# A two-block transformer kernel: the first block's TensorE order written by hand, cheaper sums, and 512-column down projections

## The chip, the cores and the metric

One core of one Trainium2 chip runs the whole program. The metric is device time in microseconds (us) of one execution. In the text PE is TensorE (PEld its weight loads), DVE is VectorE, ACT is ScalarE, POOL is GpSimd, and SP is SyncE, which here only issues DMAs. L340 is line 340 of the kernel before.

## The reference

The model works on 256 tokens of width 1024 (batch 1), all in fp32. The first block has three branches on one normed input: an RWKV-7 recurrence (8 heads of 64), a stick-breaking attention (8 heads of 64) and an attention to 256 memory rows (4 heads of 128). Their gated sum goes through an output projection, and a convolutional feed-forward of width 2816 follows. The second block is an mLSTM mixer, a feed-forward, a block attention and a third feed-forward. Cut to what the change touches:

```python
# first block
h = rms_norm(x, norm1_g)
p_rwkv, p_sb, q_mem, gate_logits = split(h @ w_in)
y_a = rwkv7_branch(p_rwkv, ...)                # a recurrence over the 256 tokens
y_b = stick_breaking_branch(p_sb, q_g, k_g)    # log_between = reversed cumsum(log_1mb) - log_1mb
y_m = memory_branch(q_mem, mem, mem_g, ...)    # softmax over the 256 memory rows
merged = sum(sigmoid(gate_logits) * einsum('btnc,ncd->btnd', stack(y_a, y_b, y_m), w_branch))
x = x + merged @ w_out
# a feed-forward: one in the first block, two in the second
hp = conv3(rms_norm(x, g) @ w_up)
x = x + (silu(gate) * val) @ w_down            # the down projection, 2816 x 1024
```

## The kernel before

Activations are held with features on partitions: a tile is 128 features by 256 tokens, and an input of width 1024 is 8 such tiles (k = 0 to 7). Every large product is done in two fp32r halves: `split` (L307) writes hi = fp32r(x) on ACT and lo = x - hi on DVE, and `mm3` (L334) adds three passes into one PSUM tile: whi with xh, whi with xl, wlo with xh (L340 to L342, 256 columns each). Products that are wanted with tokens on partitions go through `tp_group` (L356): there the activation is the stationary operand and 512 weight columns move (L363 to L365), six passes for each k, and one such step uses four weight tiles.

All weights are one stream of tiles of 128 x 128 in the order of use, eight to a DMA of 512 KB on SP's queue. `Stream.take` hands out the next tile and keeps two groups ahead: DMA into `wstg` (three buffers), then hi on ACT (L237) and lo on DVE (L238), three buffers each. The first block uses 656 tiles: memory keys and values (64), RWKV projections (112), queries, keys and values of memory and stick heads (128), then for each of three branches 8 x (8 gate + 4 branch) tiles (288) and the output projection (64). After that come up projections (352 tiles each) and down projections (176 each) of three feed-forwards, and the mixers of the second block.

The kernel is built in a framework that works out the order of each engine itself: it simulates the program and lets each engine take what it expects to be ready, with earlier program lines first. Nothing before fixes the order of PE. Semaphores follow from data, and every engine then runs its own list strictly in order.

What stands in the way of the stream in the first block: `Stats` (norms: squares are added on ACT and DVE, `_rows` L425 sums over partitions with one-column fp32 matmuls L429, `_spread` L437 copies the result over partitions with an fp32 matmul, L440); `qk_feat` (per-head norms and transposes); `run_rwkv` (for four pairs of heads `rw_prep` and `rw_scores`, then 64 x 64 triangular inverses, whose 16 x 16 diagonal blocks are solved on DVE after a trip through DRAM by DMAs of SP (L698 to L712), two doubling steps with `rw_lt`, `rw_lz`, `rw_lx`, then four chunks of the recurrence); the memory heads (`me_scores`, `me_values`); the stick heads in four pairs (L888 to L922: scores, the cumulative sum `sb_c` as three fp32 products, the weighted values `sb_o`). A plain fp32 matmul shows as two records (passes) in the trace, a transpose and an fp32r matmul as one. PSUM has eight banks in three pools: `acc` four, `pm` two, `pr` two.

The down projection is the last branch of `residual` (L939): for each of 8 output tiles `fp_tile` runs 22 x 3 passes over the separate tiles `ffh` and `ffl`, and one DVE add (L945) puts the result on the running state `xt`.

Of the kernel before, what the change touches and what calls it, by code (L numbers as in the profile page):

```python
# [16 lines left out]
T = 256  # L17
# [9 lines left out]
STARTS = (82, 148, 181, 247, 279)  # L27
HEAD = 4
# [162 lines left out]
def body(tc, a, out, voff, coff, tap=None, upto=99):  # L191
# [68 lines left out]

    warm = cpool.tile([128, 1], F32, name="warm")
# [42 lines left out]
    pw = ps_r("warm_ps")  # L304
    for _ in range(10):
        PE.matmul(pw, wz[:, 0:128], wz, start=True, stop=True)

# [26 lines left out]
    def mm3(o, X, k, w, start, stop, **kw):  # L334
        hi, lo = w
        if isinstance(X.H, list):
            xh, xl = X.H[k], X.L[k]
        else:
            xh, xl = X.H[:, k], X.L[:, k]
# [16 lines left out]
    def tp_group(X):  # L356

        po = [ps_acc(), ps_acc()]
        for k in range(KD):
            hi, lo = W.take(4)  # L360
            for tt in range(2):
                s = slice(tt * 128, (tt + 1) * 128)
                PE.matmul(po[tt], X.H[:, k, s], hi, start=(k == 0), stop=False)  # L363
                PE.matmul(po[tt], X.L[:, k, s], hi, start=False, stop=False)  # L364
                PE.matmul(po[tt], X.H[:, k, s], lo, start=False, stop=(k == KD - 1))  # L365
        return po
# [27 lines left out]
    class Stats:  # L394
# [83 lines left out]
    s4tag = dict(mkT="s4a", mv="s4b", mqT="s4c", sqT="s4d", skT="s4e", sv="s4b", macc0="s4c", macc1="f1")  # L478
# [4 lines left out]
    def qk_feat(X, st, nh, gain, name, po=None):  # L483
        po = po or tp_group(X)
        rs = head_rs(po, nh, st and st.ev, name)
        dst = s4(name)
        for tt in range(2):
            qn = normed(po, tt, rs, nh, name + "n")
            tok_to_feat(qn, dst, tt, gain)
        return dst  # L490

    def v_tok(X, st, name):
        po = tp_group(X)
        dst = s4(name).rearrange("p a t -> p (a t)").rearrange("p (a c) -> p a c", c=512)
# [3 lines left out]

    W.fill(0)
# [6 lines left out]
    pmk = tp_group(XM)  # L506
    sm._rows()
# [5 lines left out]
    for k in range(KD):  # L513
        V.scalar_tensor_tensor(x0[:, k], x0[:, k], vec("norm1_g", k), s1.bc, op0=OP.mult, op1=OP.mult)
        split(X1.H[:, k], X1.L[:, k], x0[:, k])

    mkT = qk_feat(XM, sm, 4, vec("mem_k"), "mkT", pmk)
    mv = v_tok(XM, sm, "mv")

# [67 lines left out]
    def rw_prep(p, rs, SC, BK, UV, wc):  # L587
# [28 lines left out]
        PE.matmul(pb[:, T:2 * T], con("bones"), sx, start=True, stop=True)  # L616
# [5 lines left out]
        for par in range(2):  # L622
# [5 lines left out]
            V.tensor_tensor(BK[s, p, :, o], ch(kp, par), ch(iw, par), op=OP.mult)  # L628
        pvt = ps_r("rw_pvt")
# [32 lines left out]
    def run_rwkv():  # L662
# [61 lines left out]
        for b in (16, 32):  # L724
# [6 lines left out]
            for h in range(2):  # L731
                pz = mm("rw_lz", tms[h], Zu[h])
# [3 lines left out]
                V.tensor_tensor(Zu[h], Zu[h], pz, op=OP.add)  # L736

        Y = krt[0][:, 0:4].rearrange("p c (q v) -> p c q v", v=64)
        Sw = None
        for c in range(4):  # L740
# [8 lines left out]
            A.activation(P_[64:128], pp4[64:128, :, 1], AF.Copy)  # L749
            pu = ps_r("rw_puu")  # L750
# [6 lines left out]
            A.activation(UV[64:128, :, c, 1], puv[64:128], AF.Copy)  # L757
            if c < 3:
# [30 lines left out]
            V.tensor_copy(Y[0:64, c], pp4[0:64, :, 1])  # L789

# [12 lines left out]
        YA = Half("yA", "b")  # L803
# [24 lines left out]
        return YA  # L828
# [13 lines left out]

    YA = run_rwkv()


    mqT = qk_feat(X1, None, 4, gains[:, 1:2], "mqT")
    YM = Half("yM", "a")

    def me_scores(h):
# [5 lines left out]
        for tt in range(2):  # L855
            PE.matmul(ps2[:, tt], mqT[:, h, tt * 128:(tt + 1) * 128], mkT[:, h], start=True, stop=True)
# [7 lines left out]
    def me_values(h, pr_):  # L864
        pt = ps_m("me_t")
        pt2 = pt.rearrange("p (m t) -> p m t", t=T)
        for mt_ in range(2):
            for tt in range(2):
                PE.transpose(pt2[:, mt_, tt * 128:(tt + 1) * 128], pr_[:, tt, mt_ * 128:(mt_ + 1) * 128], ident)
        pT = mp.tile([128, 2, T], F32, name="me_pT", bufs=1)  # L870
        A.activation(pT, pt2, AF.Copy)
        po_ = ps_m("me_o")
        for mt_ in range(2):
            PE.matmul(po_[:, :T], mv[:, mt_, h * 128:(h + 1) * 128], pT[:, mt_], start=(mt_ == 0), stop=(mt_ == 1))
        split(YM.H[:, h], YM.L[:, h], po_[:, :T])
        dbg(f"ym{h}", YM.H[:, h].bitcast(F32))

    sqT = qk_feat(X1, None, 8, gains[:, 0:1], "sqT")
    pr_ = me_scores(0)
    for h in range(4):  # L880
        pn_ = me_scores(h + 1) if h < 3 else None
        me_values(h, pr_)
        pr_ = pn_


    skT = qk_feat(X1, None, 8, vec("sb_k"), "skT")
    sv = v_tok(X1, None, "sv")
    YB = Half("yB", "e")  # L888
    for p in range(4):
        ze = mp.tile([128, 4, 384], F32, name="sb_ze", tag="sbt")  # L890
        z, e = ze[:, 0:2], ze[:, 2:4]
        pz = [ps_m("sb_z") for _ in range(2)]
        for tt in range(2):
            for par in range(2):
                s = slice(par * 64, (par + 1) * 64)
                PE.matmul(pz[par][:, tt * 256:256 + tt * 128], skT[s, p, tt * 128:(tt + 1) * 128], sqT[s, p, tt * 128:],  # L896
                          start=True, stop=True)
        for par in range(2):
            V.tensor_tensor(z[:, par], pz[par][:, :384], con("sbmask"), op=OP.min)
        A.activation(e, z, AF.Abs)  # L900
        A.activation(e, e, AF.Exp, scale=-1.0)
        A.activation(e, e, AF.Ln, bias=1.0)
        V.scalar_tensor_tensor(e, z, 0.0, e, op0=OP.max, op1=OP.add)
        for par in range(2):
            ep = e[:, par]
            pc = ps_m("sb_c")
            PE.matmul(pc[:, 0:256], con("negtri"), ep[:, 0:256], start=True, stop=False, skip_group_check=True)
            PE.matmul(pc[:, 128:256], con("negtri")[:, 0:1].to_broadcast([128, 128]), ep[:, 256:384], start=False, stop=True, skip_group_check=True)
            PE.matmul(pc[:, 256:384], con("negtri"), ep[:, 256:384], start=False, stop=True, skip_group_check=True)
# [371 lines left out]
```

## Time and profile before

| | us |
|---|---|
| median of 3 runs | 1152.78 |
| lowest, highest | 1152.71, 1154.36 |
| the profiled execution | 1153.26 |
| its span, first to last instruction | 1151.5 |
| VectorE, ScalarE, GpSimd busy | 862.8, 662.6, 52.8 |
| mean granted TensorE clock | 0.991 of full speed |
| HBM read | 186.46 MB, 163 GB/s over the span |

The profile is one execution. Busy time counts instructions under way; the ends of matmuls are modelled, so PE can be busy and yet not at its best, and the spacing of starts tells more than the duration of one. The chain that ended last is 92% PE. The stages by their first products: the stream starts at 6.09 us, the first product with the normed x at 35.58, the first feed-forward's up projection at 356.19, the second block at 547.59; the last matmul is at 1147.69 us.

### The profile page before, as it was taken

Reading aid. Unit: us, or ns where it says so; the run is one execution under the profiler, and the core shown is the slowest. Engines: PE = TensorE matmul, PEld = TensorE weight load, DVE = VectorE, ACT = ScalarE, POOL = GpSimd, SP = SyncE. Lnnn points to the kernel's source line nnn. Section 1 sums busy time; section 2 is a strip of 40 time slices with the busy share of each in tenths; the row PEclk is TensorE's granted clock in tenths of the full one; section 3 lists DMA queues with packets and bytes.
Section 4 is the critical chain, followed back from the end, with each engine's and each line's share of the span. In section 5 each row is a group of like instructions: output and inputs, shape, how many; then the busy total and the mean of one; then the engine's idle time right before and its main releaser. Section 6 shows DMA issues by size and latency. Waiting matters only on the chain.

```text
span 1151.5 us, 22381 instructions
## 1 busy us (share of the span) xinstructions
PE 1125.6 (98%) x8846; PEld 1069.0 (93%) x8846; DVE 862.8 (75%) x1636; ACT 662.6 (58%) x1136; POOL 52.8 (5%) x133
## 2 busy tenths in 40 slices
PE   8999879998999999999999999999999999999998
PEld 6897669887999999999979999999998899999998
DVE  7779885547666999956656779997579858999943
ACT  6765454555455766644546666665455656766632
POOL 3000000100002000000100010000010002000000
PEclk9999899998999999999999999999999999999999
DMA  8555333223566566666554556665665535556663
GB/s 286 182 151 153 92 91 94 75 74 95 180 207 200 176 187 183 178 187 189 159 166 142 175 175 187 187 180 181 188 197 172 162 113 171 181 184 184 184 202 108
DMA packets 60793, 189.35 MB, mean 164 GB/s; under 512 B 12688, under 2 KB 14992, under 8 KB 60688
## 3 DMA queue, kind: packets, MB, share of 16 engines
q1 hardware_dynamic: 59792, 186.51, 53.1%
q8 instruction: 69, 1.13, 0.4%
q0 software_dynamic: 320, 1.05, 0.3%
q10 hardware_dynamic: 576, 0.37, 0.1%
q14 instruction: 36, 0.29, 0.1%
HBM read 186.46 MB, written 1.44 MB: 163 GB/s over the span
## 4 chain that ended last, share of the span: by engine, by line
PE 92%; ACT 3%; DVE 2%; DMA 1%; issue 1%; SPq 0%; ACTq 0%
PE acc L340 24%; PE acc L341 24%; PE acc L342 24%; PE acc L363 4%; PE acc L364 4%; PE acc L365 4%; ACT whi L237 1%; DVE wlo L238 1%; PE rw_pp L745 1%; PE sb_z L896 1%; PE rw_ps L649 1%; PE tr L473 0%; DMA wstg<-in_wst_dram 0%; PE st_ps L429 0%; PE rw_lt L721 0%
## 5 line engine op out<-in xcount | busy, mean ns | idle before, releaser
L237 ACT ACTIVATE whi<-wstg 128x1024 fp32r<-128x1024 f32 (+1 forms) x453 | 374.3, 851 | 356.6 <-PE acc L341 202.8
L238 DVE TENSOR_TENSOR wlo<-wstg,whi 128x1024 fp32r<-128x1024 f32 (+1 forms) x453 | 429.6, 967 | 164.3 <-ACT whi L237 161.3
L340 PE MATMUL acc<-ffh,whi 128*128 128x256 f32 x528 | 148.6, 283 | 0.0
L341 PE MATMUL acc<-ffl,whi 128*128 128x256 f32 x528 | 148.2, 283 | 0.0
L342 PE MATMUL acc<-ffh,wlo 128*128 128x256 f32 x528 | 147.7, 283 | 0.0
L340 PEld LDWEIGHTS acc<-ffh,whi 128*128 128x128 f32 x528 | 101.2, 192 | 0.0
L341 PEld LDWEIGHTS acc<-ffl,whi 128*128 128x128 f32 x528 | 101.0, 192 | 0.0
L342 PEld LDWEIGHTS acc<-ffh,wlo 128*128 128x128 f32 x528 | 100.7, 192 | 0.0
L341 PE MATMUL acc<-x6l,whi 128*128 128x256 f32 x352 | 99.3, 284 | 0.8 <-DVE x6l L315 0.8
L340 PE MATMUL acc<-x2h,whi 128*128 128x256 f32 x352 | 99.4, 284 | 0.0
L340 PE MATMUL acc<-x6h,whi 128*128 128x256 f32 x352 | 99.3, 284 | 0.0
L340 PE MATMUL acc<-x4h,whi 128*128 128x256 f32 x352 | 99.3, 284 | 0.0
L341 PE MATMUL acc<-x2l,whi 128*128 128x256 f32 x352 | 99.3, 283 | 0.0
L341 PE MATMUL acc<-x4l,whi 128*128 128x256 f32 x352 | 99.2, 283 | 0.0
L342 PE MATMUL acc<-x2h,wlo 128*128 128x256 f32 x352 | 98.2, 283 | 0.0
L342 PE MATMUL acc<-x4h,wlo 128*128 128x256 f32 x352 | 98.1, 283 | 0.0
L342 PE MATMUL acc<-x6h,wlo 128*128 128x256 f32 x352 | 98.1, 283 | 0.0
L340 PE MATMUL acc<-x1h,whi 128*128 128x256 f32 x304 | 89.1, 294 | 3.6 <-ACT mv L496 2.0
L341 PE MATMUL acc<-x1l,whi 128*128 128x256 f32 x304 | 87.9, 290 | 0.0
L342 PE MATMUL acc<-x1h,wlo 128*128 128x256 f32 x304 | 87.0, 288 | 0.0
L1007 ACT ACTIVATE ffa<-ffu,ffcv 128x256 f32<-128x256 f32 x132 | 70.8, 588 | 0.0
L341 PEld LDWEIGHTS acc<-x6l,whi 128*128 128x128 f32 x352 | 67.5, 192 | 1.2 <-DVE x6l L315 1.2
(587 smaller groups left out, 2799.4 us busy)
## 6 DMA issues: line engine op xcount, KB each, us to landing
wstg<-in_wst_dram SPq DMA_DIRECT2D x343, 512.0 KB, 3.7
wstg<-in_wst_dram SPq DMA_DIRECT2D x4, 256.0 KB, 5.0
mst<-in_memT_dram SPq DMA_DIRECT2D x4, 256.0 KB, 5.3
x<-in_xT_dram SPq DMA_DIRECT2D x2, 512.0 KB, 7.5
xt<-in_xT_dram POOLq DMA_DIRECT2D x4, 256.0 KB, 5.6
out_dram<-xt SPq DMA_DIRECT2D x8, 128.0 KB, 3.8
cst<-in_cst_dram SPq DMA_DIRECT2D x1, 673.0 KB, 8.2
small<-in_small_dram SPq DMA_DIRECT2D x1, 512.0 KB, 9.1
```

The lines of the kernel that those rows point to most:

```text
L237: A.activation(hi[:, p], src[:, p], AF.Copy)
L238: V.tensor_tensor(lo[:, p], src[:, p], hi[:, p].bitcast(F32), op=OP.subtract)
L340: PE.matmul(o, hi, xh, start=start, stop=False, **kw)
L341: PE.matmul(o, hi, xl, start=False, stop=False, **kw)
L342: PE.matmul(o, lo, xh, start=False, stop=stop, **kw)
L363: PE.matmul(po[tt], X.H[:, k, s], hi, start=(k == 0), stop=False)
L364: PE.matmul(po[tt], X.L[:, k, s], hi, start=False, stop=False)
L365: PE.matmul(po[tt], X.H[:, k, s], lo, start=False, stop=(k == KD - 1))
L649: PE.matmul(both[par][:, c], BK[s, p, c], SC[s, p, c, par], start=True, stop=True)
L745: PE.matmul(pp4[:, q, par], SC[:, q, c, par], UV[:, q, c, par], start=(q == 0 and par == 0), stop=True, skip_group_check=True)
L896: PE.matmul(pz[par][:, tt * 256:256 + tt * 128], skT[s, p, tt * 128:(tt + 1) * 128], sqT[s, p, tt * 128:], start=True, stop=True)
L1007: A.activation(ac[:, g], u[:, g, 2:], AF.Identity, scale=cv[:, c + 2:c + 3], bias=cv[:, c + 3:c + 4])
```

## The change

A new class `Flow` counts weight tiles as they are used by `fp_tile` and `tp_group`. The small work of the first block is rewritten as generators; each `yield n` gives PE back to the stream for n more tiles (looked at on every second tile, `GRID = 2`), and `join` runs a chain to its end at once. `tc.manual_schedule` makes PE follow the program order from the first matmul to the end of the first block's output projection; other engines are ordered as before. Around it:

- Norm sums: the two halves are added on DVE first, then two one-column fp32 matmuls in place of four; the spread of a norm uses two transposes in place of two fp32 matmuls.
- The stick cumulative sum: the input is split into fp32r halves `eh`, `el` (one more ACT and DVE instruction of 128 x 768 for each pair of heads) and summed in four fp32r matmuls for a head in place of three fp32 matmuls.
- The down projections: hi and lo of an input lie side by side in one tile, so one matmul of 512 columns with whi makes both products and one of 256 columns with wlo the third; the two halves of the bank are added to `xt` in two DVE instructions.
- The mLSTM row is spread by transposes of a column (8) in place of fp32 matmuls (4), with one more row in the column transposes (`gcol`).
- The memory keys' products use the `pr` pool, ten warm-up matmuls stand at the start of the written order, and `macc1` takes the place of `mkT`.

```diff
+    class Flow:
+        n = 0
+        chains = []
+        def start(self, gen, gap=0):
+            c = [self.n + gap, gen]
+            self.chains.append(c)
+            return c
+        def step(self, c):
+            try:
+                c[0] = self.n + next(c[1])
+            except StopIteration:
+                self.chains.remove(c)
+        def tick(self, n=1):
+            for _ in range(n):
+                self.n += 1
+                if self.n % GRID == 0:
+                    for c in list(self.chains):
+                        if c[0] <= self.n:
+                            self.step(c)
+        def join(self, c):
+            while c in self.chains:
+                self.step(c)
+    flow = Flow()
...
     def fp_tile(o, X, kn=KD):
         for k in range(kn):
             mm3(o, X, k, W.take(), k == 0, k == kn - 1)
+            flow.tick()
...
     def _rows(self):
+            V.tensor_tensor(self.acc[:, 0], self.acc[:, 0], self.acc[:, 1], op=OP.add)
             for tt in range(2):
-                for j in range(2):
-                    PE.matmul(p[:, tt:tt + 1], self.acc[:, j, tt * 128:(tt + 1) * 128], ones[:, 0:1], start=(j == 0),
-                              stop=(j == 1))
+                PE.matmul(p[:, tt:tt + 1], self.acc[:, 0, tt * 128:(tt + 1) * 128], ones[:, 0:1], start=True, stop=True)
...
-                PE.matmul(pb[:, tt * 128:(tt + 1) * 128], self.rs[:, tt:tt + 1].to_broadcast([128, 128]), ident,
-                          start=True, stop=True)
+                PE.transpose(pb[:, tt * 128:(tt + 1) * 128], self.rs[:, tt:tt + 1].to_broadcast([128, 128]), ident)
...
+    def x1_chain():
+        yield 20
+        sm._rows()
+        yield 20
+        s1._rows()
+        yield 10
+        s1._spread()
+        for k in range(KD):
+            V.scalar_tensor_tensor(x0[:, k], x0[:, k], vec("norm1_g", k), s1.bc, op0=OP.mult, op1=OP.mult)
+            split(X1.H[:, k], X1.L[:, k], x0[:, k])
+    order = ExitStack()
+    order.enter_context(tc.manual_schedule(engines={mybir.EngineType.PE}))
...
+    x1c = flow.start(x1_chain())
+    pmk = tp_group(XM, ps_r)
+    flow.start(qk_feat(pmk, sm, 4, vec("mem_k"), "mkT"))
+    v_tok(XM, sm, mv)
+    flow.join(x1c)
...
 run_rwkv:
-        rw_proj(6)
+        while em.i < 6:
+            yield 1
+        yield 8
         rs = rw_norms()
         for p in range(4):
-            rw_proj(2)
-            rw_prep(p, rs, SC, BK, UV, wc)
+            while em.i < 8 + 2 * p:
+                yield 1
+            yield 6
+            yield from rw_prep(p, rs, SC, BK, UV, wc)
+            yield 8
             rw_scores(p, SC, BK, BA, RB, BKT)
...
+        yield 64
         Bu = [BAu[:, 8 * h:8 * h + 8] for h in range(2)]
...
+    ca = flow.start(run_rwkv())
+    rw_proj(14)
...
+    def memory(po):
+        yield from qk_feat(po, None, 4, gains[:, 1:2], "mqT")
+        yield 4
+        nxt = me_scores(0)
+        for h in range(4):
+            yield 10
...
+            yield 6
...
+    def sticks():
...
+        for p in range(4):
...
+            split(eh, el, e)
+            yield 24
+            for par in range(2):
+                pc = ps_m("sb_c")
+                PE.matmul(pc[:, 0:384], negtri, eh[:, par], start=True, stop=False, skip_group_check=True)
+                PE.matmul(pc[:, 0:384], negtri, el[:, par], start=False, stop=False, skip_group_check=True)
+                for x_ in (eh, el):
+                    PE.matmul(pc[:, 128:256], negtri[:, 0:1].to_broadcast([128, 128]), x_[:, par, 256:384], start=False,
+                              stop=(x_ is el), skip_group_check=True)
+                V.tensor_tensor(z[:, par], z[:, par], pc[:, :384], op=OP.add)
+            A.activation(z, z, AF.Exp)
+            yield 12
...
+        yield 4
+    cm = flow.start(memory(tp_group(X1)))
+    flow.start(qk_feat(tp_group(X1), None, 8, gains[:, 0:1], "sqT"))
+    pk = tp_group(X1)
+    csk = flow.start(qk_feat(pk, None, 8, vec("sb_k"), "skT"))
+    v_tok(X1, None, sv)
+    flow.join(csk)
+    cb = flow.start(sticks())
...
-    for n, Yn in ((2, YM), (1, YB), (0, YA)):
+    for n, chain, Yn in ((2, cm, "yM"), (1, cb, "yB"), (0, ca, "yA")):
         for m in range(KD):
             pg = ps_acc()
             fp_tile(pg[:, 0:T], X1)
             A.activation(g, pg[:, 0:T], AF.Tanh, scale=0.5)
-            fp_tile(pg[:, T:2 * T], Yn, 4)
+            flow.join(chain)
+            fp_tile(pg[:, T:2 * T], done[Yn], 4)
...
+        elif isinstance(X, list):
+            for m in range(KD):
+                ps = ps_acc()
+                for k in range(kn):
+                    hi, lo = W.take()
+                    PE.matmul(ps, hi, X[k].rearrange("p s t -> p (s t)"), start=(k == 0), stop=False,
+                              skip_group_check=True)
+                    PE.matmul(ps[:, 0:T], lo, X[k][:, 0], start=False, stop=(k == kn - 1), skip_group_check=True)
+                for j in range(2):
+                    V.tensor_tensor(xt[:, m], xt[:, m], ps[:, (1 - j) * T:(2 - j) * T], op=OP.add)
+                after_tile(m)
...
     residual(XO, ["norm2_g"], s2, [X2])
+    order.close()
...
-        PE.matmul(pm[:, :T], ident[0:4, h:h + 1].to_broadcast([4, 128]), rows[:, 2], start=True, stop=True)
+        for tt in range(2):
+            PE.transpose(pm[:, tt * 128:(tt + 1) * 128], gcol[:, 2, tt, h:h + 1].to_broadcast([128, 128]), ident)
```

## Rows read from the trace of the kernel before

**Rows 1.** page, part 1: busy us (share of the span) and instructions of TensorE

```profile
PE 1125.6 (98%) x8846; PEld 1069.0 (93%) x8846; DVE 862.8 (75%) x1636; ACT 662.6 (58%) x1136; POOL 52.8 (5%) x133
```

**Rows 2.** windows: us, busy (count) of PE, PEld, DVE, ACT, POOL, clock, DMA, GB/s

```profile
0.00:35.58 35.58, 29.78 (x127) 21.11 (x127) 28.50 (x93) 26.12 (x71) 9.19 (x32) 1.00 0.77 266
35.58:170.00 134.42, 123.86 (x759) 107.32 (x760) 107.18 (x254) 74.44 (x154) 5.83 (x19) 0.95 0.46 134
170.00:356.19 186.19, 181.60 (x1791) 171.34 (x1790) 115.39 (x185) 95.28 (x140) 8.80 (x13) 0.98 0.41 126
484.47:547.59 63.12, 63.12 (x528) 63.12 (x527) 39.42 (x55) 30.74 (x44) 2.83 (x2) 1.00 0.61 184
```

**Rows 3.** timeline of PE, four places: start us, us, instruction, count

```profile
14.46 0.95 PE L429 MATMUL st_ps<-ones,st_acc 128*128 128x1 f32 x8
...
149.77 0.60 PE L869 MATMUL me_t<-cst,me_p 128*128 128x128 f32 x4
...
848.98 0.39 PE L365 MATMUL acc<-wlo,xqh 128*128 128x512 f32 x1
...
849.89 0.39 PE L363 MATMUL acc<-whi,xqh 128*128 128x512 f32 x1
```

**Rows 4.** windows of line 340 alone, second and third stretch

```profile
35.58:170.00 134.42, 34.84 (x119) 23.47 (x119) 0.95 0.46 134
170.00:356.19 186.19, 100.25 (x346) 66.86 (x346) 0.98 0.41 126
```

**Rows 5.** timeline of VectorE, the last output tile

```profile
1148.00 0.42 DVE L945 TENSOR_TENSOR xt<-xt,acc 128x256 f32<-128x256 f32 x1 [6.36 <-PE acc L342]
```

**Rows 6.** groups of PE by line and shape: busy us, mean ns of one

```profile
L429 PE MATMUL st_ps<-ones,st_acc 128*128 128x1 f32 x56 | 6.7, 238 | 0.0
...
L856 PE MATMUL me_s<-mkT,mqT 128*128 128x256 f32 x16 | 5.2, 454 | 0.0
...
L1086 PE MATMUL ml_pm<-ml_rows,cst 4*128 4x256 f32 x8 | 2.8, 426 | 0.0
```

**Rows 7.** timeline of PE, the last pair of stick heads

```profile
253.08 0.92 PE L896 MATMUL sb_z<-sqT,skT 64*128 64x256 f32 x4
...
260.75 0.67 PE L907 MATMUL sb_c<-sb_ze,cst 128*128 128x256 f32 x2 [1.24 <-DVE rw_mean L794]
...
261.70 0.60 PE L907 MATMUL sb_c<-sb_ze,cst 128*128 128x256 f32 x2
...
267.68 0.49 PE L340 MATMUL acc<-yB,whi 128*128 128x256 f32 x1 [0.49 <-ACT yB L311]
```

**Rows 8.** waits of PE, 35.58 to 170 us: total, times, longest

```profile
PE me_o L874 <- ACT me_pT L871: 3.3, 3, 1.5
PE me_t L869 <- DVE yM L312: 2.1, 1, 2.1
...
PE rw_pb L616 <- DVE rw_f L615: 1.9, 1, 1.9
PE rw_ps L649 <- DVE rw_bk L628: 1.6, 1, 1.6
```

**Rows 9.** timeline of PE, the first norm: spread and first product

```profile
25.65 0.61 PE L440 MATMUL st_pb<-cst,s_rs 128*128 128x128 f32 x4
...
35.58 0.49 PE L340 MATMUL acc<-x1h,whi 128*128 128x256 f32 x1 [2.03 <-ACT mv L496]
```

**Rows 10.** timeline of VectorE, SP and PE at the solves; last row: SP's waits

```profile
135.37 0.42 DVE L654 TENSOR_TENSOR rw_ba<-rw_ps,cst 64x256 f32<-64x256 f32 x1
...
161.17 3.86 SPq L709 DMA_DIRECT2D rw_z<-dz  x8
165.07 7.71 SPq L712 DMA_DIRECT2D rw_krv<-dz  x14
...
175.45 2.08 PE L721 MATMUL rw_lt<-rw_krv,rw_ba 64*64 64x64 f32 x60
...
SPq L231 <- DVE wlo L238: 634.4, 233, 14.2
```

More of the change, by code (lines that the diff above doesn't have):

```diff
@@ L27 @@
 STARTS = (82, 148, 181, 247, 279)
+GRID = 2
 HEAD = 4
@@ L497, in v_tok @@
         return dst
+    def x1_chain():
[10 more added lines that the diff above has]
+    order.enter_context(tc.manual_schedule(engines={mybir.EngineType.PE}))
+    pw = ps_r("warm_ps")
+    for _ in range(10):
+        PE.matmul(pw, wz[:, 0:128], wz, start=True, stop=True)
     W.fill(0)
@@ L628, in rw_prep @@
             V.tensor_tensor(BK[s, p, :, o], ch(kp, par), ch(iw, par), op=OP.mult)
+        yield 14
+        PE.matmul(pb[:, T:2 * T], con("bones"), sx, start=True, stop=True)
         pvt = ps_r("rw_pvt")
@@ L862, in me_scores @@
         return pr_
[L864 to L867, printed above, removed]
-            for tt in range(2):
[L869 to L893, printed above, removed]
+    def memory(po):
+        yield from qk_feat(po, None, 4, gains[:, 1:2], "mqT")
+        YM = done["yM"] = Half("yM", "a")
+        yield 4
+        nxt = me_scores(0)
+        for h in range(4):
+            yield 10
+            pr_ = nxt
+            pt = ps_m("me_t")
+            pt2 = pt.rearrange("p (m t) -> p m t", t=T)
+            for mt_ in range(2):
+                for tt in range(2):
+                    PE.transpose(pt2[:, mt_, tt * 128:(tt + 1) * 128], pr_[:, tt, mt_ * 128:(mt_ + 1) * 128], ident)
+            pT = mp.tile([128, 2, T], F32, name="me_pT", bufs=1)
+            A.activation(pT, pt2, AF.Copy)
+            if h < 3:
+                nxt = me_scores(h + 1)
+            yield 6
+            po_ = ps_m("me_o")
+            for mt_ in range(2):
+                PE.matmul(po_[:, :T], mv[:, mt_, h * 128:(h + 1) * 128], pT[:, mt_], start=(mt_ == 0), stop=(mt_ == 1))
+            split(YM.H[:, h], YM.L[:, h], po_[:, :T])
+            dbg(f"ym{h}", YM.H[:, h].bitcast(F32))
+        yield 4
@@ new lines, in sticks @@
+    def sticks():
+        YB = done["yB"] = Half("yB", "e")
+        ehl = mp.tile([128, 4, 384], F32R, name="sb_e", tag="f1")
+        eh, el = ehl[:, 0:2], ehl[:, 2:4]
+        negtri = mp.tile([128, 128], F32R, name="sb_nt")
+        A.activation(negtri, con("negtri"), AF.Copy)
+        for p in range(4):
+            ze = mp.tile([128, 4, 384], F32, name="sb_ze", tag="sbt")
+            z, e = ze[:, 0:2], ze[:, 2:4]
+            pz = [ps_m("sb_z") for _ in range(2)]
+            for tt in range(2):
+                for par in range(2):
+                    s = slice(par * 64, (par + 1) * 64)
+                    PE.matmul(pz[par][:, tt * 256:256 + tt * 128], feat["skT"][s, p, tt * 128:(tt + 1) * 128],
+                              feat["sqT"][s, p, tt * 128:], start=True, stop=True)
+            for par in range(2):
+                V.tensor_tensor(z[:, par], pz[par][:, :384], con("sbmask"), op=OP.min)
+            A.activation(e, z, AF.Abs)
+            A.activation(e, e, AF.Exp, scale=-1.0)
+            A.activation(e, e, AF.Ln, bias=1.0)
+            V.scalar_tensor_tensor(e, z, 0.0, e, op0=OP.max, op1=OP.add)
+            split(eh, el, e)
+            yield 24
+            for par in range(2):
+                pc = ps_m("sb_c")
[7 more added lines that the diff above has]
+            yield 12
+            po_ = ps_m("sb_o")
@@ L903, in body @@
[L903 to L909, printed above, removed]
-            V.tensor_tensor(z[:, par], z[:, par], pc[:, :384], op=OP.add)
@@ L911, in body @@
-        A.activation(z, z, AF.Exp)
-        po_ = ps_m("sb_o")
-        for par in range(2):
-            s = slice(par * 64, (par + 1) * 64)
-            h = 2 * p + par
-            PE.matmul(po_[s, 0:256], sv[:, 0, h * 64:(h + 1) * 64], z[:, par, 0:256], start=True, stop=False,
-                      skip_group_check=True)
-            PE.matmul(po_[s, 128:256], sv[:, 1, h * 64:(h + 1) * 64], z[:, par, 256:384], start=False, stop=True,
-                      skip_group_check=True)
-        split(YB.H[:, p], YB.L[:, p], po_[:, :T])
@@ L1061, in body @@
     V.tensor_scalar(rows[:, 2], gM, -1.0, None, op0=OP.mult)
-    gcol = mp.tile([128, 2, 2, 4], F32, name="ml_gcol")
+    gcol = mp.tile([128, 3, 2, 4], F32, name="ml_gcol")
     pc = ps_m("ml_pc")
-    pcv = pc[:, 0:16].rearrange("p (r a h) -> p r a h", r=2, h=4)
-    for r in range(2):
+    pcv = pc[:, 0:24].rearrange("p (r a h) -> p r a h", r=3, h=4)
+    for r in range(3):
         for tt in range(2):
```

82 lines of the change are left out of this document (33 added, 49 removed).

## The prediction

> **What bounds the kernel now.** I read the page first, then the windows by stage, then the spacing of single matmuls, then the waits. The page has TensorE (PE) busy for 1125.6 of 1151.5 us [rows 1]. A busy PE only says that some matmul is under way, so the next question is where it is idle or slow. The windows answer it. In the down projection of the first feed-forward, from 484.47 us, it is busy all of 63.12 us at clock 1.00, the 2.4 GHz level: 528 passes, 63.12 / 528 = 0.120 us each. In the first block it is idle for 35.58 - 29.78 = 5.8, 134.42 - 123.86 = 10.6 and 186.19 - 181.60 = 4.6 us in the three stretches up to 356.19 us, 21.0 together, and the clock of the second and third is 0.95 and 0.98, worth 0.05 x 134.42 = 6.7 and 0.02 x 186.19 = 3.7 us [rows 2]. So after 356 us only less matmul work saves time; before it order could give back up to 21.0 + 10.4 = 31 us (an upper end, since slow clock and idle partly coincide).
>
> How much of the first block is weight stream? A pass of 256 columns takes the 0.120 us above, one of 512 takes (849.89 - 848.98) / 4 = 0.2275 us [rows 3]. The third stretch has 346 passes of line 340, one for each weight tile, so 346 x 3 x 0.120 = 124.6 us; the second has 119, so 42.8 us [rows 4], and by the code 128 tiles of token projections in 192 wide passes, 43.7 us. The rest (186.2 - 124.6 - 4.6 = 57.0 and 134.4 - 86.5 - 10.6 = 37.3 us) is small matmuls and slow clock. The written order removes none of these matmuls, it only places them.
>
> **The change part by part.**
>
> **Down projections.** There are three, each 176 weight tiles (528 passes), so 528 tiles. A tile costs 3 x 0.120 = 0.360 us now; after, one pass of 512 and one of 256 columns, 0.2275 + 0.120 = 0.3475: 12.5 ns x 528 = 6.6 us less. At 2.4 GHz 256 columns are 106.7 ns and 512 are 213.3, so both rows hold 13 to 14 ns beyond their columns, and that is what is saved once a tile. Lower end: 0, if the swap of shapes eats it. Upper end: after a wide pass the narrow one might fall to the spacing of one-column passes, (0.95 - 0.24) / 7 = 0.10 us [rows 3, 6]: 32.5 ns x 528 = 17 us. I take 6.6, which both shapes' own rows give. All of it is on the path, since PE is idle for 0 us there. VectorE gets a second add of 0.42 us for each of 24 output tiles; it is busy 39.42 of 63.12 us in that stretch [rows 2], so 23 are covered; the last is behind the last matmul [rows 5]: +0.4. The next stage's last input is as much later twice; I put +0.5 for both (0 to 2).
>
> The Trainium skill, "TensorE: Matmul & The Clock Gate", section "Back-to-back issue gap", gives a warm matmul a fixed cost of some 2.5 ns beyond its columns; by it the three projections would give back only 2.5 ns x 528 = 1.3 us (an estimate from that page). The trace has 13 to 14 ns at both widths, so the rows decide; the page's outcome is like rival B below.
>
> **Fewer passes for sums.** Seven norm sums of 8 one-column passes each (x56 [rows 6]) take 8 x 0.10 = 0.80 us; half of it goes, 0.40 x 5 = 2.0 us after the first block and 0.8 in it. The VectorE add put ahead of each, 0.42 us by an add of that shape [rows 5], runs beside the weight stream, since an evacuation wants the sum and not PE; without that cover it is 7 x 0.42 = 2.9 us. Five spreads go from 4 passes (x4 [rows 9]) to 2 transposes, both at some (0.60 - 0.27) / 3 = 0.11 us [rows 3]: 0.2 x 4 = 0.9 us, and 0.2 in the block. The mLSTM row spread, 8 passes busy 2.8 us [rows 6], becomes 8 transposes, 0.9 us, and two tiny ones: -1.7 us (0.5 to 1.9). One half of the stick sum takes 0.95 us now (260.75 to 261.70 [rows 7]), eight halves 7.6 us. After: two passes of 384 columns (between 0.120 and 0.2275, so 0.174 us) and two of 128, which no row shows in this type: 0.11 us like a transpose, or as much as 0.2275. That is 4.5 to 6.4 us, a saving of 1.2 to 3.1; I take 2.0.
>
> Outside the first block: -6.6 + 0.4 + 0.5 - 2.0 - 0.9 - 1.7 = -10.3 us. Inside, as matmul work: -0.8 - 0.2 - 2.0 = -3.0 us.
>
> **The written order.** Before, PE took whatever the planner saw ready; now a small matmul that waits holds all weight passes behind it. I followed the counter of weight tiles through the code. Most steps are 4 to 24 tiles apart (1.4 to 8.6 us) for chains of two to five short operations. So the waits of the memory heads (3.3 + 2.1) and inside the recurrence's pairs (1.9 + 1.6), most of the second stretch's 10.6 us [rows 8], should go. Three places are not plainly covered.
>
> First, the start: the spread of the first norm moves from 25.65 us to the 52nd of 64 tiles, near 30 us at the pace of the first stretch. Eight splits follow, which took at most 35.58 - 25.65 = 9.9 us; PE starts on the first of them, and its wait of 2.0 us for a bank [rows 9] goes, as the memory keys leave that pool. I put 0 (-2 to +4).
>
> Second, tile 306: the first inverse product (rw_lt) needs the small triangular solves. From the last mask product at 135.37 to the bulk of rw_lt at 175.45 it is 40 us now, with 22 of 24 reload DMAs in the two rows of SP [rows 10]. The order allows 64 tiles, 64 x 6 x 0.2275 / 4 = 21.8 us, and beside them the heads' scores (5.2 us busy [rows 6]), as many value products, and transposes: 34 us. I price the wait at 6.
>
> Third, tile 408: the stick chain starts at tile 304 and is to step at 306, 330, 342, 366, 378, 402, 414, 438, 450, but the second branch calls for its end after one gate of 8 tiles, at 408. What remains, above all the whole fourth pair, is then issued with no tile between. That pair's chain is in the trace: scores at 253.08, sums at 260.75, first use at 267.68, 14.6 us [rows 7]. PE's own work in it is about 0.9 + 1.1 + 0.9 us, so 12 us idle, and I add 2 for the slower clock that now goes with the idle of such stretches [rows 2].
>
> New idle against old: start 5.8 and 5.8; second stretch 6 + 2 for small new waits, against 10.6; third 12 + 1 against 4.6; the clock gives back 6 of 10.4 and takes 2. Together -2.6 + 8.4 - 6 + 2 = +1.8. With -3.0 the first block ends 1.2 us earlier.
>
> **Sum.** The profiled execution took 1153.26 us, its span 1151.5 and 1.8 around it; it lies 0.5 above the median of the runs. 1153.3 - 10.3 - 1.2 - 0.5 = 1141 us.
>
> **Rivals.**
>
> A, the order pays: VectorE, busy 107.18 of 134.42 us in the second stretch [rows 2], gets its inputs early enough that neither the solves nor the fourth stick pair is waited for long. Then the 31 us go but for the start's 5.8, a tail of 5 and 3 of small waits: 17. For it: the idle of rows 2 lies just where the order is rewritten. Against: the call at tile 408 leaves nothing between the steps. 1152.8 - 10.3 - 3 - 17 = 1122 us.
>
> B, the wide pass saves next to nothing: the 13 ns are not per matmul. For it: no row has the two shapes in turn. Against: the same excess at both widths. 1.3 in place of 6.6 us: 1146 us.
>
> C, slower: the solves at tile 306. SP serves its queue in order, and a weight load on it waits 634.4 / 233 = 2.7 us for its buffer. Now the 24 reloads run nearly unbroken (161.17 to 172.78 [rows 10]), because PE takes few weights then. With PE kept on weights, a load can stand between every few of them; six such, 16 us, make PE wait 22 us in place of 6. From 12 us on top it is slower than before. Against: loads are issued up to three buffers ahead. 1141 + 16 = 1157 us.
>
> **How the numbers follow.** Forecast 0.53, A 0.23, B 0.13, C 0.11. The likeliest has its own range of 1131 to 1149 (down projections 0 to 17, start and tail some 5 either way). The overall range of 1118 to 1152 holds A and B and leaves out C and a little of each end. About 0.2%, 2.3 us, is what a measurement of this kernel can tell from no change. Faster: 0.49 + 0.23 + 0.11 = 0.83; the same 0.06; slower 0.11.
>
> **What would show it.** The first x2h product (at 356.19 now) should start near 355; at 336 it is A, at 371 C. After the first gate of the second branch PE should sit idle for about 12 us before its first yB product, in two or three waits (for the split ahead of the sums, and for the exponential ahead of the output). rw_lt should show a wait of some 6 us. A down projection should take 61 us and not 63.1; 62.7 is B. A norm sum should have 4 passes in 0.4 us. The prediction fails if the tail at tile 408 is short, or if the block's small matmuls, 37.3 and 57.0 us with their slow clock, shrink by themselves once they stand in another order.

## The result and the profile after

The changed kernel takes 1189.8 us (median of 4 runs, 1188.5 to 1191.1) against 1153.6 for the kernel before: 1.031 times as long, interval 1.0295 to 1.0331. The forecast was 1141 us, faster; it was wrong in sign. The profiled execution took 1190.39 us, its span is 1188.5.

The page of the kernel after, answering to [rows 1]; the second and third line are its strip of 40 slices:

```profile
PE 1121.6 (94%) x8266; PEld 1038.9 (87%) x8266; DVE 879.0 (74%) x1671; ACT 668.7 (56%) x1141; POOL 53.3 (4%) x133
...
PE   8999788886888999999999999999999999999998
...
PEclk9989888987999999999999999999999999999999
```

TensorE has less work than before (1121.6 against 1125.6 us) and is idle for 66.9 us in place of 25.9. Both the holes and the slow clock lie in the first third. The windows by the same stages as [rows 2] (first x1h product, arrival at the solves, first x2h product), then one down projection, and last the tail of the stick heads, from their last scores to the first product with yB; columns as there:

```profile
0.00:37.46 37.46, 30.64 (x125) 20.69 (x125) 28.76 (x92) 26.70 (x70) 8.60 (x31) 1.00 0.75 262
37.46:176.45 138.99, 123.83 (x748) 106.81 (x746) 106.34 (x256) 76.49 (x157) 7.75 (x19) 0.93 0.38 112
176.45:404.16 227.71, 188.30 (x1779) 175.27 (x1779) 123.01 (x191) 99.24 (x143) 7.70 (x13) 0.93 0.35 112
531.52:592.89 61.37, 61.37 (x354) 53.54 (x353) 41.93 (x62) 30.91 (x45) 2.79 (x2) 1.00 0.61 189
278.42:292.44 14.02, 5.17 (x23) 3.64 (x23) 7.96 (x18) 6.78 (x7) 0.00 (x0) 0.59 0.10 37
```

The first block ends at 404.16 us, 48.0 later than before. Everything behind it takes 1188.5 - 404.16 = 784.3 us against 1151.5 - 356.19 = 795.3, so 11.0 less. The loss is all in the first block, most of it in the third stretch: PE is idle for 39.4 us there (4.6 before), at clock 0.93 (0.98). In the second it is idle for 15.2 us (10.6 before), at 0.93 (0.95). What PE waited for up to 404.16 us (total, times, longest):

```profile
PE acc L364 <- ACT gt L1004: 28.3, 22, 4.4
PE sb_c L966 <- ACT sb_e L338: 7.0, 1, 7.0
PE tr L497 <- DVE mqTn L487: 5.7, 1, 5.7
PE tr L497 <- DVE skTn L487: 3.3, 1, 3.3
PE tr L497 <- DVE sqTn L487: 2.9, 1, 2.9
...
PE sb_o L978 <- ACT sb_ze L972: 1.5, 1, 1.5
```

The first row is new, and it is the largest. It belongs to the gates: 24 output tiles, each a product of 8 weight tiles (gate, into the lower half of a bank `pg`), ScalarE's tanh on it (L1004, tile gt), and a product of 4 weight tiles (branch, into the upper half of the same bank). The timeline of the kernel after, all engines, at one of them:

```profile
323.82 0.28 PE L366 MATMUL acc<-x1h,wlo 128*128 128x256 f32 x1
324.13 0.38 ACT L1004 ACTIVATE gt<-acc 128x256 f32<-128x256 f32 x1 [0.50 <-PE acc L366]
324.57 0.19 PEld L364 LDWEIGHTS acc<-yB,whi 128*128 128x128 f32 x1 [0.68 <-ACT gt L1004]
324.57 0.38 PE L364 MATMUL acc<-yB,whi 128*128 128x256 f32 x1 [0.47 <-ACT gt L1004]
...
324.79 0.28 PE L365 MATMUL acc<-yB,whi 128*128 128x256 f32 x1
```

The last gate pass starts at 323.82 and ends, by the profile's modelled duration, at 324.10. The branch pass needs nothing from the tanh, yet it starts only at 324.57, after the tanh is through with the other half of its bank: 0.75 us from pass to pass in place of 0.12. Where ScalarE is busy with something else the wait is longer. The worst one, on ScalarE and then on PE:

```profile
196.01 1.28 ACT L960 ACT_TABLE_LOAD   x1
197.31 0.84 ACT L960 ACTIVATE sb_ze<-sb_ze 128x768 f32<-128x768 f32 x1
198.17 1.28 ACT L1004 ACT_TABLE_LOAD   x1
199.46 0.38 ACT L1004 ACTIVATE gt<-acc 128x256 f32<-128x256 f32 x1
...
199.90 0.58 PE L364 MATMUL acc<-yM,whi 128*128 128x256 f32 x1 [3.97 <-ACT gt L1004]
```

A step of the stick chain (L960) got in ahead of the tanh, each of the two with a table load of 1.28 us, and PE stood for 3.97 us.

The kernel before has the same bank, the same tanh and the same dependency. Its timeline, all engines, at such a place:

```profile
252.87 0.28 PE L342 MATMUL acc<-x1h,wlo 128*128 128x256 f32 x1
253.08 0.73 PEld L896 LDWEIGHTS sb_z<-sqT,skT 64*128 64x128 f32 x4
253.08 0.92 PE L896 MATMUL sb_z<-sqT,skT 64*128 64x256 f32 x4
253.19 0.38 ACT L932 ACTIVATE gt<-acc 128x256 f32<-128x256 f32 x1 [0.19 <-PE acc L342]
253.93 0.19 PEld L341 LDWEIGHTS acc<-yB,whi 128*128 128x128 f32 x1
```

The free order put the stick scores behind the gate's last pass; elsewhere it interleaved passes of another output tile. The tanh ran in their shadow, and that kernel's waits of PE list no tanh at all.

The tail at tile 408 is there as the forecast described it. PE, kernel after, fourth pair of stick heads:

```profile
278.42 0.92 PE L954 MATMUL sb_z<-sqT,skT 64*128 64x256 f32 x6 [1.34 <-DVE yB L339]
286.36 0.69 PE L966 MATMUL sb_c<-sb_e,sb_nt 128*128 128x384 f32 x1 [7.03 <-ACT sb_e L338]
...
290.95 1.12 PE L978 MATMUL sb_o<-sb_ze,sv 128*64 128x256 f32 x4 [1.52 <-ACT sb_ze L972]
...
292.44 0.58 PE L364 MATMUL acc<-yB,whi 128*128 128x256 f32 x1
```

### The profile page after: what moved, and what is told of

Same layout as the page of the kernel before. It is cut to its first block, busy times and chain, and to the rows that moved or that the text cites. A ratio compares the mean times of both kernels' runs of the same rounds, so it can differ in the third digit from the quotient of the medians.

```text
span 1188.5 us, 21261 instructions
## 1 busy us (share of the span) xinstructions
PE 1121.6 (94%) x8266; PEld 1038.9 (87%) x8266; DVE 879.0 (74%) x1671; ACT 668.7 (56%) x1141; POOL 53.3 (4%) x133
## 4 chain that ended last, share of the span: by engine, by line
PE 75%; ACT 2%; DVE 2%; issue 1%; ACTq 0%
PE acc L364 16%; PE acc L365 16%; PE acc L366 16%; PE acc L1043 10%; PE acc L1045 5%; PE acc L390 2%; PE acc L388 2%; PE acc L389 2%; ACT whi L238 1%; DVE wlo L239 1%; ACT gt L1004 0%; PE tr L497 0%; PE mb_s L1286 0%; PE rw_pp L792 0%; PE mb_o L1315 0%
## 5 line engine op out<-in xcount | busy, mean ns | idle before, releaser
L1043 PE MATMUL acc<-ffy,whi 128*128 128x512 f32 x528 | 183.2, 395 | 0.0
L1045 PE MATMUL acc<-ffy,wlo 128*128 128x256 f32 x528 | 144.5, 278 | 0.0
L1043 PEld LDWEIGHTS acc<-ffy,whi 128*128 128x128 f32 x528 | 98.0, 188 | 22.0
L1045 PEld LDWEIGHTS acc<-ffy,wlo 128*128 128x128 f32 x528 | 99.3, 188 | 1.4
L365 PEld LDWEIGHTS acc<-x2l,whi 128*128 128x128 f32 x352 | 67.6, 192 | 0.0
L364 PEld LDWEIGHTS acc<-x2h,whi 128*128 128x128 f32 x352 | 67.6, 192 | 0.0
```

The source lines that it names most:

```text
L1043: PE.matmul(ps, hi, X[k].rearrange("p s t -> p (s t)"), start=(k == 0), stop=False, skip_group_check=True)
L1045: PE.matmul(ps[:, 0:T], lo, X[k][:, 0], start=False, stop=(k == kn - 1), skip_group_check=True)
```

## The experiments

The theory after the result, T: the written order puts gate and branch of one output tile back to back, so each branch product waits for the tanh on its own bank, 28 us of waits and some 10 us of slow starts and slow clock with the holes. Rivals: PE is held by what ScalarE and VectorE can deliver, whatever it waits for (R1); the loss lies ahead of the gates, in the transposes that wait for VectorE and in the slow clock (R2); it comes with the new sequence of program lines or with the other edits of the first block (R3). Ratios are to the kernel before, run beside each group (median 1154.7 us for runs 1 to 4, 1154.1 for 5 to 8, 1153.8 for 9 and 10).

**1. A bank of its own for the branch product** (changed kernel; the two uses of the upper half of `pg` read `pb`)

```diff
-            fp_tile(pg[:, T:2 * T], done[Yn], 4)
+            pb = ps_acc()
+            fp_tile(pb[:, 0:T], done[Yn], 4)
```

> The changed kernel with one edit: the branch product gets a PSUM bank of its own, in place of the second half of the gate's bank. Theory T (the written order makes PE wait at each of the 24 gate tiles until ScalarE's tanh has read the bank that the next product is to write): the waits put on the tanh, 28.3 us in 22 places, go, with some 3 us of slow starts behind them and up to 7 us of slow clock: 1190 falls to 1151 to 1158. Rival R1 (PE is held by what ScalarE and VectorE can deliver in these stages, whatever waits for it): other waits take the place, 1175 to 1190. Rival R2 (the loss is in front of the gates, in the transposes that wait for VectorE and in the slow clock): 1180 or more.

1152.1 us (ratio to before 0.998, 0.996 to 1.000): 37.7 us less than the changed kernel, for one line of allocation. The third stretch of this kernel, to be held against 176.45:404.16, and its largest waits:

```profile
173.16:363.53 190.37, 176.39 (x1780) 167.56 (x1780) 121.31 (x191) 98.66 (x143) 7.70 (x13) 0.96 0.43 134
```

```profile
PE sb_c L966 <- ACT sb_e L338: 7.0, 1, 7.0
PE tr L497 <- DVE mqTn L487: 5.7, 1, 5.7
...
```

PE's idle time there falls from 39.4 to 14.0 us, and no wait for gt is left. T holds for the bulk, and R1 and R2, which expected 1175 and more, do not. But the first block ends at 363.53, still 7.3 us later than before.

**2. The changed kernel in a free order**

```diff
-    order.enter_context(tc.manual_schedule(engines={mybir.EngineType.PE}))
```

> The changed kernel without the written order: PE's order is left to the planner again; the generators only set the order of the program lines. Theory T (all of the loss comes with the fixed order, and everything else of the change is a gain): 1153.6 - 10.5 behind the first block - 1 to 3 in it: 1139 to 1143. Rival R3 (the loss comes with the new sequence of program lines or with the other edits of the first block, such as the added splits of the stick sum): 1155 to 1190.

1160.9 us (1.0054, 1.0036 to 1.0073). The gt waits went here too, so the bank costs only in the written order; but T's 1139 to 1143 was missed by 18 us, as R3 had it. This kernel's last score product of the recurrence (rw_ps) starts at 144.9 us (135.2 in run 8, which has the same edits in the program sequence of before) and rw_lt at 182.9 (169.1). A likely reading is that the program lines, regrouped for the counter, also steer the planner and make the recurrence late. It was not tried by itself, and the other edits of the first block (warm-up, pools, the place of `macc1`) were not taken apart from it.

**3. The 512-column down projections alone, on the kernel before**

```diff
-                fp_tile(ps[:, :T], X, kn)
+                for k in range(kn):
+                    hi, lo = W.take()
+                    PE.matmul(ps, hi, X[k].rearrange("p s t -> p (s t)"), start=(k == 0), stop=False, ...)
+                    PE.matmul(ps[:, 0:T], lo, X[k][:, 0], start=False, stop=(k == kn - 1), ...)
```

> The kernel before with the 512-column down projections alone. All theories: they are worth what the three stretches of the changed kernel show, 63.1 - 61.4 = 1.7 us each, 5 us in all, 1148.5; if the wide pass is worth 12.5 ns a tile as forecast, 1147.

1150.7 us (0.996, 0.994 to 0.998): 0.004 x 1154.7 = 4.6 us less, near the 5 expected; the interval, 2 to 7 us, does not tell 5 from the 6.6 of the forecast.

**4. The written order ended ahead of the first gate** (changed kernel)

```diff
+    order.close()
     mh = [s4("macc0"), s4("macc1")]
...
-    order.close()
```

> The changed kernel with the written order closed ahead of the first gate, after the 304 tiles of projections. Theory T: the waits on the tanh and the forced tail of the stick heads (some 10 us of waits) go, the front's loss stays (the first inverse product starts at 176 in place of about 166 us): 1148 to 1155. Rival R2 (the front is where the loss is): 1175 or more.

1150.8 us (0.997, 0.995 to 0.999). Bank and neighbours as in the changed kernel, only PE's order free from tile 304 on: the loss is gone as in run 1. It takes both, the shared bank and the fixed order. One part of the expectation failed: the wait at the tail, which was to go, is still there.

```profile
PE sb_c L966 <- ACT sb_e L338: 6.2, 1, 6.2
```

Run 2, with no written order at all, has 6.8 us of it, and run 8, in the program sequence of before, 0.5. So the tail does not come from the fixed order alone; it goes with what runs 2 and 4 share and run 8 lacks, above all the new sequence of program lines.

**5. Run 1 with the stick chain closer**, so that no step is left at tile 408

```diff
             split(eh, el, e)
-            yield 24
+            yield 16 if p else 22
...
             A.activation(z, z, AF.Exp)
-            yield 12
+            yield 6
```

> The changed kernel with the branch product in its own bank, and the stick chain closer: 16 to 22 weight tiles ahead of the sums in place of 24, 6 ahead of the output in place of 12, so that its last step is issued before tile 408. Theory T (the tail at tile 408 is priced as it was: sb_c waits 7.0 us and sb_o 1.5, and the clock is low for some 10 us behind it): the two waits go, 8 to 11 us less than with the bank alone (1152.1), so 1141 to 1145. Rival U (the tail is no loss of its own: the stick chain is bound by VectorE and ScalarE, and closer steps turn into waits inside the chain): the 8.5 us come back as waits of the sb_c or sb_o products of earlier pairs, and the time is 1149 to 1154.

1147.9 us (0.994, 0.992 to 0.996), 4.2 less than run 1 (0.4% by the ratios); neither side's range. The sb_c waits fall from 7.0 to 3.2 us (1.8 + 1.4), but rw_py now waits 3.4 us for the recurrence's normed rows, which was hidden in the tail. The first block ends at 363.07 in the profiled execution, hardly sooner; as the profiled executions of runs 1 and 5 took nearly the same time (1149.68 and 1149.45 us), their traces do not show where the 4.2 us of the medians lie.

**6. Run 5 with the transposes of mqT, sqT and skT 28, 26 and 26 tiles behind their products**

```diff
-        yield 16
+        yield GAP.get(name, 16)
```

> As the run with the closer stick chain, and the transposes of the memory queries, stick queries and stick keys come 28, 26 and 26 weight tiles behind the products' end in place of 16. Theory T (these transposes wait because VectorE is full from 90 to 120 us and 16 tiles are too few; mqTn 5.7, skTn 3.3, sqTn 3.0 us): 6 to 12 us less than the closer chain alone, so 1130 to 1139 if that gives its 8 to 11. Rival U (VectorE is the bound of the stretch; what it does later is waited for elsewhere, at the solves or at the memory heads): under 3 us less, the waits show at me_s, me_t or rw_lt.

1147.6 us (0.995, 0.994 to 0.997): nothing gained, as U says. What the kernel now waits for up to 364 us, and the product that waits:

```profile
PE rw_lt L767 <- DMA rw_krv<-dz: 8.8, 2, 5.3
PE rw_py L865 <- DVE rw_krv L853: 3.4, 1, 3.4
PE sb_c L967 <- ACT sb_e L338: 1.8, 1, 1.8
PE tr L497 <- DVE mqTn L487: 1.8, 1, 1.8
```

```profile
166.81 0.44 PE L767 MATMUL rw_lt<-rw_krv,rw_ba 64*64 64x64 f32 x2 [5.28 <-DMA rw_krv<-dz]
170.81 3.64 PE L767 MATMUL rw_lt<-rw_krv,rw_ba 64*64 64x64 f32 x62 [3.56 <-DMA rw_krv<-dz]
```

The 5.7 + 3.3 + 3.0 us of the transposes shrank to 1.8, PE came to tile 306 at 166.81 - 5.28 = 161.5 us, where run 5 came at 176.9, and there it waited 8.8 us for the reloads of the solves. The chain ahead of rw_lt (VectorE's solves, 24 small DMAs) moves less than PE: the bulk of rw_lt starts at 170.81 here and at 176.85 in run 5, 6 us earlier where PE came 15 us earlier. (It is 175.45 before [rows 10] and 175.01 in run 7.) More than half of what PE saves ahead of it is handed back there.

**7. The kernel before with the edits that lie behind the first block**, no written order: run 3's edit, and

```diff
+            V.tensor_tensor(self.acc[:, 0], self.acc[:, 0], self.acc[:, 1], op=OP.add)
...
+                PE.matmul(p[:, tt:tt + 1], self.acc[:, 0, tt * 128:(tt + 1) * 128], ones[:, 0:1], start=True, stop=True)
...
+                PE.transpose(pb[:, tt * 128:(tt + 1) * 128], self.rs[:, tt:tt + 1].to_broadcast([128, 128]), ident)
...
+            PE.transpose(pm[:, tt * 128:(tt + 1) * 128], gcol[:, 2, tt, h:h + 1].to_broadcast([128, 128]), ident)
```

> The kernel before with the edits that lie behind the first block: 512-column down projections, two passes in place of four for a norm sum, transposes for the spreads of the norms and of the mLSTM row; no written order. By the terms of the prediction -10.3 us outside the first block (the trace of after shows -11.0) and -1 inside it: 1142 to 1145 against 1154.7. Rival: the small edits give nothing in a free order, and only the 4.6 us of the down projections show: 1149 to 1151.

1142.2 us (0.9904, 0.9889 to 0.9918), as expected. It beats both kernels. Its first block ends at 355.23, 1.0 earlier than before; that much is not clear of scatter, for run 3, which leaves the block as it was, ends it at 357.08. One of its down projections:

```profile
482.59:543.96 61.37, 61.37 (x355) 53.54 (x353) 41.93 (x62) 30.91 (x45) 2.80 (x2) 1.00 0.62 190
```

**8. Run 7 with the stick sums in fp32r halves**

```diff
         V.scalar_tensor_tensor(e, z, 0.0, e, op0=OP.max, op1=OP.add)
+        split(eh, el, e)
...
-            PE.matmul(pc[:, 0:256], con("negtri"), ep[:, 0:256], start=True, stop=False, ...)
+            PE.matmul(pc[:, 0:384], negtri, eh[:, par], start=True, stop=False, ...)
+            PE.matmul(pc[:, 0:384], negtri, el[:, par], start=False, stop=False, ...)
```

> As the run with the edits behind the first block, and the stick sums split into fp32r halves, in the free order and the program sequence of before. By the prediction 1.2 to 3.1 us less than without the split: 1140 to 1143. Rival (what made the changed kernel in a free order 6 us slower than before is the split: one more step of ScalarE and VectorE in each pair's chain, and half of VectorE's work of the third stretch behind it): 4 to 18 us more, 1147 to 1162, with the first block's end later and waits at sb_c.

The run also lets `macc1` take the place of `mkT`, as the changed kernel does, because the halves take its own. 1144.9 us (0.9928, 0.9913 to 0.9943): 2.7 us more than run 7, not less, and between the two forecasts. The passes themselves are cheaper, as the forecast said. PE's sums of the third pair of heads (times of the second passes, both halves):

```profile
227.19 0.34 PE L910 MATMUL sb_c<-sb_e,sb_nt 128*128 128x384 f32 x1
227.36 0.34 PE L912 MATMUL sb_c<-sb_e,sb_nt 128*128 128x128 f32 x2
227.53 0.39 PE L910 MATMUL sb_c<-sb_e,sb_nt 128*128 128x384 f32 x1
```

A 384-column pass is 0.17 us and the two of 128 columns 0.17 together, so a half takes some 0.51 us against 0.95 [rows 7]: eight halves save 3.5 us of PE. But the split puts one more ScalarE and one more VectorE instruction into every pair's chain. These groups of the same kernel give the price (min/median/max ns):

```profile
L311 ACT ACTIVATE sb_e<-sb_ze x4: 843/846/846, 200.2 to 265.0; 128x768 fp32r<-128x768 f32 x4
L312 DVE TENSOR_TENSOR sb_e<-sb_ze,sb_e x4: 947/954/959, 201.1 to 266.1; 128x768 fp32r<-128x768 f32 x4
```

0.85 + 0.95 = 1.8 us a pair, 7.2 us for four. PE itself waits for the split's tiles for only 0.5 us. But the pairs run later and later: the last scores of the fourth start at 257.30 (253.04 in run 7), its sums at 265.86 (261.94). There PE runs dry, and the clock falls as it does not in run 7. The stretch in run 7, then in run 8:

```profile
260.00:270.00 10.00, 7.92 (x61) 6.91 (x59) 8.83 (x20) 5.45 (x8) 0.00 (x0) 1.00 0.17 52
```

```profile
260.00:270.00 10.00, 6.58 (x27) 5.18 (x26) 8.17 (x19) 7.43 (x8) 0.00 (x0) 0.65 0.17 52
```

That the longer chain is the cause, and not the new place of `macc1`, fits these times, but the two were not tried apart. Run 8 is still some 15 us below run 2 by the ratios, so the split is a small part of R3.

**9 and 10. Sixteen of the 24 reloads on POOL's queue** (in run 7, and in run 6)

```diff
-                nc.sync.dma_start(X[h][r, :, j], dz[0, b, 8 * h:8 * h + 8]...)
+                nc.gpsimd.dma_start(X[h][r, :, j], dz[0, b, 8 * h:8 * h + 8]...)
```

> The kernel before with the edits that lie behind the first block (1142.2), and the 16 reloads of the inverses' first operand issued on POOL's DMA queue, beside the 8 of rw_z that stay on SP's. Theory S (the stretch between the solves and rw_lt is a serial chain of 24 small DMAs on one queue, 11.6 us from 161.17 to 172.78 in the trace of before, while PE is idle for some 7 of 20 us and its clock drops): the chain is 4 to 6 us shorter and the first block ends 3 to 6 us earlier, 1136 to 1140. Rival V (the DMAs themselves or POOL's issue take as long): within 1 us of 1142.

> The written order with own banks, closer sticks and longer gaps (1147.6), and the same 16 reloads on POOL's queue. There PE sits at tile 306 from about 161 to 172 us, with rw_lt waiting for the last reload. Theory S: the reloads end 5 to 6 us earlier, the wait at rw_lt falls from 8.8 to about 3 us, and the time to 1140 to 1143. Rival V: the wait stays and the time is 1146 to 1149.

1146.5 us (0.993, 0.990 to 0.996) and 1145.1 us (0.992, 0.990 to 0.995). On run 7 it is worse, if anything, and outside both forecasts; on run 6 it is 2.5 us better at intervals that overlap, between the two forecasts, and the wait at rw_lt stays at 8.4 us. The two fail in different places. In run 10 the answer is in the issues and landings. Its POOL queue:

```profile
156.34 4.96 POOL L757 DMA_DIRECT2D rw_krv<-dz  x9 [36.97 <-DMA dz<-rw_xb]
162.12 3.65 POOL L757 DMA_DIRECT2D rw_krv<-dz  x7 [0.81 <-DMA rw_krv<-dz]
```

POOL needs 4.96 / 9 = 0.55 us for each. The last one is issued at 165.8 in place of 169.7 us, but lands later after its issue (3.5 us in place of 1.9, medians of the DMA view), and the bulk of rw_lt starts at 169.72 in place of 170.81: 1.1 us of the 5 to 6 that S expected.

In run 9 the reloads did come earlier: the last starts at 167.9 us in place of 172.3 (run 7), and its queue's longest landing is 3.7 us, so all should be in by some 172. But in the planner's free order PE is busy with other products, most of them weight passes, until it starts the bulk of rw_lt at 177.53, later than the 175.01 of run 7:

```profile
177.53 2.08 PE L719 MATMUL rw_lt<-rw_krv,rw_ba 64*64 64x64 f32 x60
```

So run 9 says nothing against the second queue itself: there PE's order left the earlier reloads unused.

## Why the prediction was wrong

**The step that failed** is the passage "Most steps are 4 to 24 tiles apart ... So the waits of the memory heads and inside the recurrence's pairs should go. Three places are not plainly covered". It followed only the steps that the counter spaces. The gates are not among them: they are the stream itself, and the diff leaves them as they were. Yet a fixed order changes them most. Before, the planner had always something to put between a gate's last pass and its branch's first; the written order may put a small step at every second tile, and nothing has to stand at that seam. So the sum has "third 12 + 1" us of idle PE for a stretch that showed 39.4. The text says that "a small matmul that waits holds all weight passes behind it"; the largest wait was that of a weight pass itself. The gates' waits, priced at nothing, are 28.3 us. With the clock they cost 37.7 us (1189.8 to 1152.1 in run 1), of the 48.0 by which the first block ends later. Runs 1, 2 and 4 take the wait away in three ways. Whether it is the bank in the hardware or the framework's tracking of one PSUM tile that asks for the wait was not separated.

The Trainium skill, "Perfetto Trace Analysis", section "Matmuls", says that independent matmul groups should rotate through different PSUM banks so that the evacuation of one overlaps the next. The trace agrees, at up to 4.4 us a place; the kernel before broke that rule and shows no wait for the tanh, because the order hid it.

**Behind the first block: right.** -10.3 us forecast, -11.0 measured (-10.9 in run 7). A down projection gives back 63.12 - 61.37 = 1.75 us, 9.9 ns a tile where 12.5 was forecast, so 5.3 in place of 6.6 us. Rival B, 62.7 us a stretch, is refuted by the 61.37. The formula behind its 1.3 us (the Trainium skill, "TensorE: Matmul & The Clock Gate", section "Back-to-back issue gap") is given there for an isolated matmul and not for a stream of them, so B was never that section's figure for this case. The small edits and the second adds make up the other -5.7 us, where -4.6 + 0.9 = -3.7 was forecast; no run takes them apart.

**The start: in its bounds.** First x1h product at 37.46, +1.9 us (0, -2 to +4).

**Tile 306: no wait in the changed kernel, but one behind it.** PE reached it late, at 176.4 us, and waited for nothing. In run 6, with the other waits removed or cut, 8.8 us of waiting stand at rw_lt; 6 were forecast. Rival C is not seen: no weight load stands between the reloads, neither in the changed kernel nor in run 6.

**The tail at tile 408: seen, smaller than forecast.** From the last scores (278.42) to the first yB product (292.44) PE is idle for 14.02 - 5.17 = 8.9 us, in the two waits foretold and small ones; 12 were forecast. The reason given, that the call at tile 408 forces it, is only part: the wait for sb_e stays in runs 2 and 4, in a free order. Cutting it was worth less than its waits (run 5); rw_py's wait of 3.4 us took some of their place.

**Missed beside the gates:** the transposes of mqT, sqT and skT, 16 tiles behind their products, wait 11.9 us for VectorE. The rows had its load (107.18 of 134.42 us [rows 2]) and the forecast used it in rival A alone.

**First-block matmul work, -3.0 us:** the 1.0 of the sums and spreads is not shown apart from scatter (run 7). The stick split came out 2.7 us slower (run 8) where 2.0 were to be gained: the forecast priced its passes on PE and not the two instructions that it adds to each pair's chain.

**The clock.** The written order was to win 6 us of slow clock and lose 2. The mean fell from 0.991 to 0.977; the tail from 278.42 us, with PE busy for 5.17 of 14.02, has 0.59, near the 1.2 GHz level. The second and third stretch are at 0.93, which by the forecast's own measure costs 0.07 x 139.0 + 0.07 x 227.7 = 25.7 us in place of its 10.4 - 6 + 2 = 6.4. The clock was low where the holes are, and the holes were forecast too few.

**What the order is worth:** run 6 has the written order with its three kinds of wait taken out or cut, run 8 nearly the same edits in a free order: 1147.6 against 1144.9 us, at intervals that overlap. A hand-written order, repaired this far, buys nothing here. The solves alone do not explain it: the bulk of rw_lt starts 5.0 us earlier in run 6 (170.81 against 175.77), and still its block ends 3.3 us later (361.09 against 357.82). From rw_lt to the recurrence's next product, rw_lz, and from there to the block's end, run 6, then run 8:

```profile
170.81:180.84 10.03, 8.90 (x86) 7.25 (x86) 1.81 (x3) 1.36 (x3) 0.00 (x0) 0.70 0.32 105
180.84:361.09 180.25, 172.43 (x1696) 164.07 (x1696) 117.44 (x188) 97.68 (x142) 7.84 (x13) 0.97 0.41 130
```

```profile
175.77:180.49 4.72, 4.72 (x84) 4.36 (x83) 2.48 (x4) 1.32 (x3) 0.00 (x0) 1.00 0.23 57
180.49:357.82 177.33, 173.02 (x1675) 163.49 (x1675) 116.58 (x187) 96.59 (x140) 7.75 (x13) 0.97 0.42 130
```

The head start is lost at once: nearly the same PE work takes 10.0 us in place of 4.7, at clock 0.70 right behind the 8.8 us of waiting. Later PE is idle for 7.8 us against 4.3. The best kernel of the study is run 7.

## What to carry to other kernels

When an engine's order is fixed by hand, walk the whole instruction list and ask at every seam what the next instruction waits for, above all at the lines that are not edited: a dependency that a free order hid becomes a wait. Where nothing stands between them, two products that are evacuated at different times belong in different PSUM banks. And a wait removed ahead of a serial chain on other engines is in large part handed on to that chain's end (in run 6, 8.8 of 15 us): find it first.

## What was not expected of the hardware

- ScalarE's table loads, 1.28 us each, stood ahead of a stick step and of the tanh behind it (196.01 and 198.17 us); with PE's order fixed both lay in one wait of PE of 3.97 us.
- A second DMA queue shortened the issue of a chain of small reloads by some 4 us, but not the landing: 3.5 us in place of 1.9 in run 10, where the product that waits for it came 1.1 us earlier, and 2.3 in place of 2.0 in run 9.
